# Sums of the retention heads taken on chip instead of reloaded, sums of the up layers on one engine, and a later start of the adaLN sums

## The chip, the cores and the metric

The kernel runs on one NeuronCore of a Trainium2 chip. The core has a matrix engine (TensorE, PE in the profile), three engines for elementwise work (VectorE: DVE; ScalarE: ACT; GpSimd: POOL), a SyncE (SP) that here only issues DMAs, and 16 DMA engines that move data between HBM and on-chip memory. Each engine works through its own instructions in order; engines wait for each other by semaphores. A DMA that an engine issues stands in that engine's instruction order. Matmul results land in PSUM, in 8 banks of 128x512 floats. The metric is the device time of one execution in microseconds (us), lower is better.

## What is computed

Two layers of a diffusion backbone on 1024 latent tokens of width 1024 with 256 context tokens, in float32. Cut to what the change touches:

```python
# layer 0: retention mixer (4 heads, key width 256, value width 512), then SwiGLU
o_f = retention_chunk_scan(qx, kx, vx, lg_f, s_f)            # chunks of 128 tokens
o_b = flip(retention_chunk_scan(flip(qx), flip(kx), flip(vx), lg_b, s_b))
o = o_f + o_b
o = o * rsqrt(mean(o * o, axis=-1) + EPS)                    # per head
yx = (silu(g) * o) @ w_o                                     # (1024, 2048) @ (2048, 1024)
hx = hx + g1 * yx
fx = rms_norm(hx, norm_ffn) * (1 + sc2) + sh2
hx = hx + g2 * ((silu(fx @ w1) * (fx @ w3)) @ w2)
# layer 1: the same with a gated short convolution as mixer
# sh, sc, g of both layers: silu(c) @ ada_w + ada_b  (adaLN)
return rms_norm(hx, final_norm)
```

## The kernel before, in words

**Arithmetic.** Every float32 operand is split into a high and a low part (`split`, L123 to L126: a ScalarE copy, then a subtraction on VectorE), and a product is three fast matmuls (`mm3`, L128 to L132). Most large products use a seven-product scheme of the Strassen and Winograd kind: of the four quarters of the activation, x11, x12, x21, x22, seven operands are made, three of them quarters themselves and four sums, numbered 5 (x12 - x11), 6 (x22 - that sum), 7 (sum 6 - x11) and 4 (x21 - sum 6).

**Order of the work.** The program is written as one order of TensorE work. Beside it a queue of small steps (`hooks`) is emptied one step after each product or half step, and a scheduler then places the instructions of each engine; the numbers on the tiles are names only.

**Retention stage (about 600 to 855 us).** It runs over 4 heads, and in each over 10 steps (2 of context, 8 chunks of 128 tokens), forward and backward together. `update` adds k^T v to the state in PSUM and copies it out as high and low parts: L723 on ScalarE, then L724 on VectorE. `read` multiplies queries with that copy. So every step has a round trip from TensorE to ScalarE to VectorE and back to TensorE. When a head has ended, eight `finish` steps (one for each chunk c) go through `hooks`: L769 on VectorE scales the chunk with the gate, 4 transposes on TensorE (L774) turn it, L776 on ScalarE copies it from PSUM, and L778, a DMA issued by ScalarE, stores it to `og_d[h][c // 4]` in pieces of 512 bytes.

**The sums of the heads.** The output projection `w_o` is such a seven-product layer (`down`). Its quarters: head h is 2p + i with p the pair of heads, i the first or second half of the inner dimension, and j = c // 4 the token half. In the kernel before, `o_steps` makes the four sums: `load` (L1409) reads the stored tiles back with SyncE's DMAs, `one` (L1416) and `other` (L1421, L1423, L1425) subtract on VectorE, and `put` (L1412) stores the sums to `x_d` by ScalarE's DMAs, in pieces of 2 KB. These steps are queued behind the `finish` steps of a head. `down` then reads its operands one by one (L1106, three ahead) and splits them.

**Up layers (three of them, from about 1045, 1690 and 2025 us).** `modulator` makes the normalized operands (L294, L303, then `split`); every third of them has its subtraction (L126) on GpSimd. `x_sums` makes the four sums of the seven-product scheme (L412, L416); for the odd ones of four tiles the subtractions run on GpSimd (their splits on VectorE). `winograd` makes the weights' sums (L452 to L458), and L496, L500, L506 add up products from PSUM. The first phase of the program uses `x_sums` too. `x_steps` (L1241 to L1251) makes the sums of what an up layer puts out, two tile pairs at a time, through `hooks`.

**adaLN.** `ada_next` forms scale, shift and gate vectors as row sums on VectorE (L203), two instructions of 512 columns a step, with weights loaded two steps ahead; `also` calls it after every third product of the first up layer, from its first product on.

Of the kernel before, what the change touches and what calls it, by code (L numbers as in the profile page):

```python
# [17 lines left out]
P = 128  # L18
# [33 lines left out]
def hybrid_kernel(ctx: ExitStack, tc: tile.TileContext, a: dict):  # L52
# [353 lines left out]
    def x_sums(xc, b, kt):  # L406

        x11, x12, x21, x22 = (b[kt + 4 * i, j] for i in range(2) for j in range(2))
        eng = nc.gpsimd if kt % 2 else nc.vector

        def step(n, dst, p, q):
            eng.tensor_sub(dst, p, q)  # L412
            x_parts(xc, n, kt, dst)

        def seven():
            eng.tensor_sub(x21, x21, x12)  # L416
            step(7, x12, x12, x11)

        return {
            5: lambda: step(5, x12, x12, x11),  # L420
            6: lambda: step(6, x12, x22, x12),
            7: seven,
            4: lambda: x_parts(xc, 4, kt, x21),
        }
# [97 lines left out]
    og_d = spilled("og_d", HEADS, NTB, shape=(P, 4, 512))  # L522
    x_d = spilled("x_d", 7, FT // 2)
# [242 lines left out]
    def finish(h, c):  # L766
# [6 lines left out]
        for b in range(4):  # L773
            nc.tensor.transpose(ot[:, b * P : (b + 1) * P], gt[:, b * P : (b + 1) * P], ident)  # L774
        og = ttile()
        nc.scalar.copy(og, ot)  # L776
        t0 = (c % 4) * P
        nc.scalar.dma_start(  # L778
            og_d[h][c // 4][:, :, t0 : t0 + P], og.rearrange("p (b t) -> p b t", b=4)
        )  # L780
        gate(h, c + G_AHEAD)

    def og_of(k, tb):
        return og_d[k // 4][tb][:, k % 4]
# [437 lines left out]
    def x_steps(n_pairs):  # L1222
# [8 lines left out]
        def take(pr, i, j, t):  # L1231
# [3 lines left out]
            if all((pr, i, j) in parts for i in range(2) for j in range(2)):  # L1235
# [18 lines left out]
                hooks.extend([one, two])  # L1254
# [3 lines left out]
    def modulator(xs, s, sh):  # L1258
        def one(kt, tb, rb):
# [3 lines left out]
                nc.gpsimd if kt % 3 == 1 else nc.vector,  # L1263
# [24 lines left out]
    def ffn(i, xs, w_plain, consume, order, then=(), last=False):  # L1288
# [18 lines left out]
        def also():  # L1307
            n = next(count)
            if i == 0 and n == 0:
                ada_load(ADA_EARLY)  # L1310
                ada_load(ADA_EARLY + 1)
            elif n % 3 == 0:
# [73 lines left out]

    o_ready = set()
    o_sums = {}

    def o_tile(i, n):  # L1390

        k, tb = S_X[n]
        return og_of(i // 4 * 8 + k * 4 + i % 4, tb)

    def o_src(n, i):
        if n in S_X:
            return o_tile(i, n) if (i // 4 * 2 + S_X[n][0]) in o_ready else None
        return x_d[n - 1][i] if (n, i) in o_sums else None

    def o_steps(pairs):  # L1400


        t = {}

        def load(i, k):
            r = raw()
            for tb in range(NTB):
                t[i, k, tb] = r[:, tb * TB : (tb + 1) * TB]
                nc.sync.dma_start(t[i, k, tb], og_of(i // 4 * 8 + k * 4 + i % 4, tb))  # L1409

        def put(n, i, src):
            nc.scalar.dma_start(x_d[n - 1][i], src)  # L1412
            o_sums[n, i] = True

        def one(i):
            nc.vector.tensor_sub(t[i, 0, 1], t[i, 0, 1], t[i, 0, 0])  # L1416
            put(5, i, t[i, 0, 1])

        def other(i):
            x11, x12, x21, x22 = (t.pop((i, k, tb)) for k in range(2) for tb in range(NTB))  # L1420
            nc.vector.tensor_sub(x22, x22, x12)  # L1421
            put(6, i, x22)
            nc.vector.tensor_sub(x11, x22, x11)  # L1423
            put(7, i, x11)
            nc.vector.tensor_sub(x21, x21, x22)  # L1425
            put(4, i, x21)

        def after_loads(k, f):

            todo = [lambda i=i: load(i, k) for i in pairs] + [nothing] * 2  # L1430
            sums = [nothing] * 2 + [lambda i=i: f(i) for i in pairs]

            def both(x, y):
                x()
                y()

            return [lambda x=x, y=y: both(x, y) for x, y in zip(todo, sums)]

        return after_loads(0, one), after_loads(1, other)

    o_steps = {h: o_steps(range(2 * h, 2 * h + 4)) for h in (0, 2)}
# [6 lines left out]
    for i, (r, _) in enumerate(seq):  # L1448
# [8 lines left out]
        if r is not None and r[1] == steps - 1:  # L1457
# [6 lines left out]
            hooks.append(lambda h=h: o_ready.add(h))  # L1464
            if h:
                hooks.extend(o_steps[h // 2 * 2][h % 2] if h > 1 else sum(o_steps[0], []))
# [189 lines left out]
```

## Time and profile before

| what | value |
|---|---|
| time, median of 3 runs | 2673.85 us (2672.15 to 2674.78) |
| the profiled execution's own time | 2677.7 us |
| span in its profile, first to last instruction | 2675.9 us |
| mean granted TensorE clock | 0.987 |
| busy: PE, DVE, ACT, POOL | 97%, 73%, 44%, 8% of the span |
| HBM traffic | 317.07 MB read, 111.67 MB written |

Times inside the program are us from the span's start. Busy time of TensorE counts each matmul with its drain, which overlaps the next one, so gaps show better in the number of matmuls in a window than in busy time. In a row of a timeline the brackets say how long the engine had been idle before it and what ended that. PEclk is the granted clock as a share of the full one.

### The profile page before, as it was taken

The numbers are of one execution on the slowest core, as the hardware profiler recorded it, in microseconds if no ns is written. First come the engines' busy times: TensorE is split into PE (matmuls) and PEld (weight loads), VectorE is DVE, ScalarE is ACT, GpSimd is POOL, SyncE is SP. The second block draws the span as 40 slices with busy tenths as digits, with TensorE's granted clock in tenths as the row PEclk, the third lists the DMA queues.
The fourth block names the chain that finished last, engine by engine and source line by source line (L and its number), as shares of the span: only waits on it lengthen the run. The fifth ranks groups of instructions, "written<-read, shape, count | busy, mean of one in ns | idle before, by whom it ended". The sixth has DMA issues, their size and how long they took to land.

```text
span 2675.9 us, 32892 instructions
## 1 busy us (share of the span) xinstructions
PE 2589.0 (97%) x11448; PEld 2111.6 (79%) x11448; DVE 1952.4 (73%) x3354; ACT 1187.8 (44%) x2162; POOL 203.0 (8%) x142
## 2 busy tenths in 40 slices
PE   8999999999978899999999999999998999999998
PEld 4788888887767687788888888788777888888886
DVE  4886766768877878877766877777798566667774
ACT  4643333448866345333333445433354333334452
POOL 1110221002210002000000000200002000000000
PEclk9999999999999899999999999999999999999998
DMA  9556234664679743445545734123552233328532
GB/s 328 193 165 220 79 115 165 230 227 126 207 252 309 270 127 96 156 146 179 189 132 197 266 102 152 34 81 97 177 197 73 87 110 107 101 98 305 166 98 83
DMA packets 212614, 430.93 MB, mean 161 GB/s; under 512 B 22624, under 2 KB 40160, under 8 KB 212448
## 3 DMA queue, kind: packets, MB, share of 16 engines
q1 hardware_dynamic: 139248, 318.92, 37.1%
q10 hardware_dynamic: 73200, 109.91, 11.2%
q8 instruction: 90, 1.47, 0.2%
q14 instruction: 76, 0.62, 0.1%
HBM read 317.07 MB, written 111.67 MB: 160 GB/s over the span
## 4 chain that ended last, share of the span: by engine, by line
PE 80%; DVE 8%; DMA 6%; issue 3%; ACT 2%; POOL 0%; SPq 0%; ACTq 0%; DVEq 0%; POOLq 0%
PE ps L130 26%; PE ps L131 26%; PE ps L132 26%; DVE u L126 3%; ACT u L125 1%; DMA raw<-in_w_kc 1%; DMA raw<-og_d 1%; DMA tt<-x_d 1%; DMA og_d<-tt 1%; PE ps L954 1%; DVE tt L412 1%; DVE t L294 0%; DMA tt<-in_cxT 0%; PE ps L774 0%; DVE u L724 0%
## 5 line engine op out<-in xcount | busy, mean ns | idle before, releaser
L130 PE MATMUL ps<-u 128*128 128x512 f32 x3472 | 1366.4, 394 | 46.1 <-DVE u L724 18.0
L131 PE MATMUL ps<-u 128*128 128x512 f32 x3472 | 1363.2, 393 | 1.7 <-DVE u L126 1.5
L132 PE MATMUL ps<-u 128*128 128x512 f32 x3472 | 1359.3, 392 | 0.0
L130 PEld LDWEIGHTS ps<-u 128*128 128x128 f32 x3472 | 656.1, 189 | 194.7 <-DVE u L724 21.0
L131 PEld LDWEIGHTS ps<-u 128*128 128x128 f32 x3472 | 656.9, 189 | 142.0 <-DVE u L126 6.0
L132 PEld LDWEIGHTS ps<-u 128*128 128x128 f32 x3472 | 656.7, 189 | 136.7 <-issue 0.5
L125 ACT CAST u<-raw 128x512 fp32r<-128x512 f32 x772 | 466.4, 619 | 563.9 <-PE ps L132 273.6
L126 DVE TENSOR_TENSOR u<-raw,u 128x512 fp32r<-128x512 f32 x772 | 539.5, 712 | 163.1 <-ACT u L125 161.3
L125 ACT CAST u<-tt 128x512 fp32r<-128x512 f32 x394 | 232.1, 619 | 241.1 <-issue 58.5
L126 DVE TENSOR_TENSOR u<-tt,u 128x512 fp32r<-128x512 f32 x391 | 280.0, 743 | 79.8 <-ACT u L125 77.8
L493 ACT COPY tt<-ps 128x512 f32<-128x512 f32 x174 | 101.9, 586 | 212.1 <-PE ps L132 206.4
L724 DVE SCALAR_TENSOR_TENSOR u<-ps,u 128x512 fp32r<-128x512 f32 x128 | 84.7, 685 | 26.6 <-ACT u L723 26.3
L506 DVE TENSOR_TENSOR tt<-tt,ps 128x512 f32<-128x512 f32 x58 | 39.9, 687 | 87.0 <-PE ps L132 87.0
L126 POOL TENSOR_TENSOR u<-t,u 128x512 fp32r<-128x512 f32 x15 | 21.4, 1428 | 1032.0 <-ACT u L125 1031.2
L1202 DVE SCALAR_TENSOR_TENSOR t<-ps,ada,t 128x512 f32<-128x512 f32 x80 | 56.1, 751 | 53.6 <-PE ps L132 53.6
L723 ACT ACTIVATE u<-ps 128x512 fp32r<-128x512 f32 x128 | 72.9, 597 | 39.8 <-PE ps L132 21.7
L673 POOL TENSOR_TENSOR u<-t,u 128x512 fp32r<-128x512 f32 x40 | 55.0, 1378 | 327.2 <-ACT u L672 179.9
L500 DVE TENSOR_TENSOR tt<-tt,ps 128x512 f32<-128x512 f32 x58 | 39.8, 686 | 49.1 <-ACT tt L493 48.9
L203 DVE SCALAR_TENSOR_TENSOR raw<-raw,c_row 128x512 f32<-128x512 f32 x84 | 55.2, 689 | 23.9 <-DMA raw<-in_ada_t 23.9
L130 PE MATMUL ps<-u,kh 128*128 128x512 f32 x144 | 58.2, 404 | 1.2 <-POOL u L673 1.2
L131 PE MATMUL ps<-u,kh 128*128 128x512 f32 x144 | 57.0, 396 | 0.5 <-DVE kh L683 0.5
L132 PE MATMUL ps<-u,kh 128*128 128x512 f32 x144 | 56.9, 395 | 0.0
(147 smaller groups left out, 1797.2 us busy)
## 6 DMA issues: line engine op xcount, KB each, us to landing
tt<-x_d SPq DMA_DIRECT2D x214, 256.0 KB, 3.7
raw<-in_w SPq DMA_DIRECT2D x88, 512.0 KB, 4.0
x_d<-tt ACTq DMA_DIRECT2D x130, 256.0 KB, 2.6
raw<-in_w SPq DMA_DIRECT2D x88, 256.0 KB, 5.1
raw<-in_ada_t SPq DMA_DIRECT2D x42, 512.0 KB, 5.2
t<-in_ada_t SPq DMA_DIRECT2D x76, 256.0 KB, 4.8
raw<-in_w_v SPq DMA_DIRECT2D x36, 512.0 KB, 5.0
x_d<-t ACTq DMA_DIRECT2D x52, 256.0 KB, 3.4
```

The costliest lines, as they stand in the source:

```text
L125: nc.scalar.copy(dst_hi, src)
L126: (eng or nc.vector).tensor_sub(dst_lo, src, dst_hi.bitcast(F32))
L130: nc.tensor.matmul(ps, w_hi, x_lo, start=first, stop=False, **kw)
L131: nc.tensor.matmul(ps, w_lo, x_hi, start=False, stop=False, **kw)
L132: nc.tensor.matmul(ps, w_hi, x_hi, start=False, stop=last, **kw)
L203: nc.vector.scalar_tensor_tensor(w[e], w[e], 1.0, c_row[:, k], op0=ALU.mult, op1=ALU.mult, accum_out=sums[:, e, ct : ct + 1],)
L493: nc.scalar.copy(m[p, n], ps)
L506: nc.vector.tensor_add(t, t, ps)
L673: nc.gpsimd.tensor_sub(t[:, 1], v, t[:, 0].bitcast(F32))
L723: nc.scalar.activation(s[:, 0], st[d][m], AF.Copy, scale=f)
L724: nc.vector.scalar_tensor_tensor(s[:, 1], st[d][m], f, s[:, 0].bitcast(F32), op0=ALU.mult, op1=ALU.subtract,)
L1202: nc.vector.scalar_tensor_tensor(h, banks[which][c], gate[:, kt : kt + 1], h, op0=ALU.mult, op1=ALU.add)
```

## The change

It does four things.

1. `finish` keeps the turned chunks of the first three quarters of a pair of heads on chip (`o_place`, six `raw` tiles of a pool of 38 for each pair) and subtracts as soon as the chunk that completes a sum is there: `first` (one subtraction a chunk, after the second token half of an even head), `others` (three a chunk, after the second token half of an odd head). The sums are stored to a new `os_d`, in pieces of 512 bytes, by ScalarE. The store of a sum is put off to the next chunk's `finish`. Tiles that nobody loads any more (quarter x12) are not stored, and `o_steps` with its 32 loads is gone.
2. `x_sums` and `modulator` use VectorE for all their tiles.
3. The first two steps of `x_steps` of an up layer are put off by four products (`[nothing] * 4`).
4. `also` starts the second part of the adaLN sums with product 12 instead of 0.

```diff
     def x_sums(xc, b, kt):
-        eng = nc.gpsimd if kt % 2 else nc.vector
         def step(n, dst, p, q):
-            eng.tensor_sub(dst, p, q)
+            nc.vector.tensor_sub(dst, p, q)
             x_parts(xc, n, kt, dst)
         def seven():
-            eng.tensor_sub(x21, x21, x12)
+            nc.vector.tensor_sub(x21, x21, x12)
...
+    os_d = spilled("os_d", 4, HEADS // 2, shape=(P, 4, 512))
...
-        og = ttile()
+        og, put = o_place(h, c)
         nc.scalar.copy(og, ot)
-        t0 = (c % 4) * P
-        nc.scalar.dma_start(
-            og_d[h][c // 4][:, :, t0 : t0 + P], og.rearrange("p (b t) -> p b t", b=4)
-        )
+        t = slice((c % 4) * P, (c % 4 + 1) * P)
+        def store(dst, src):
+            nc.scalar.dma_start(dst[:, :, t], src.rearrange("p (b t) -> p b t", b=4))
+        if (h % 2, c // 4) != (0, 1):
+            store(og_d[h][c // 4], og)
+        o_finish()
+        if put is not None:
+            o_late.append(lambda: put(store))
         gate(h, c + G_AHEAD)
...
+    o_parts, o_late = {}, []
+    def o_finish():
+        while o_late:
+            o_late.pop()()
+    def o_place(h, c):
+        p, i, j, c4 = h // 2, h % 2, c // 4, c % 4
+        if (i, j) == (1, 1):
+            og = ttile()
+        else:
+            if c4 % 2 == 0:
+                o_parts[p, "r"] = raw()
+            og = o_parts[p, "r"][:, (c4 % 2) * 512 : (c4 % 2 + 1) * 512]
+            o_parts[p, i, j, c4] = og
+        def first(store):
+            x11 = o_parts[p, 0, 0, c4]
+            nc.vector.tensor_sub(x11, og, x11)
+            store(os_d[0][p], x11)
+        def others(store):
+            t1, x12, x21 = (o_parts.pop((p, *k, c4)) for k in ((0, 0), (0, 1), (1, 0)))
+            nc.vector.tensor_sub(t1, og, t1)
+            store(os_d[1][p], t1)
+            nc.vector.tensor_sub(x12, og, x12)
+            store(os_d[2][p], x12)
+            nc.vector.tensor_sub(x21, x21, t1)
+            store(os_d[3][p], x21)
+        return og, {(0, 1): first, (1, 1): others}.get((i, j))
...
-                hooks.extend([one, two])
+                hooks.extend([nothing] * (4 if pr == 0 else 0) + [one, two])
...
-                nc.gpsimd if kt % 3 == 1 else nc.vector,
+                nc.vector,
...
-            if i == 0 and n == 0:
+            if i == 0 and n == 12:
                 ada_load(ADA_EARLY)
                 ada_load(ADA_EARLY + 1)
-            elif n % 3 == 0:
+            elif n > 12 and n % 3 == 0:
                 ada_next()
...
-    def o_steps(pairs):
...
-    o_steps = {h: o_steps(range(2 * h, 2 * h + 4)) for h in (0, 2)}
...
-            hooks.append(lambda h=h: o_ready.add(h))
-            if h:
-                hooks.extend(o_steps[h // 2 * 2][h % 2] if h > 1 else sum(o_steps[0], []))
+            hooks.extend([o_finish, lambda h=h: o_ready.add(h)])
```

**Three places in the engines' order.** Line numbers of the changed kernel stand in its rows: L780 is the store in `finish` (L778 before), L816, L818, L820 are the subtractions of `others`, L495 is L496 before, L451 to L457 are L452 to L458, L1283 and L1287 are L1244 and L1248.

ScalarE at the `finish` steps of head 1, between two pairs of state copies (L723). Before:

```order
L723 ACTIVATE u<-ps 128x512 x2
L672 CAST u<-t_6413 128x512
L682 ACTIVATE kh<-tt,kdec 128x256
L125 CAST u<-tt 128x512
L776 COPY tt<-ps 128x512 x2
L778 DMA og_d_1_218<-tt 512x1x128 x2
L747 ACTIVATE t_6629<-ps,odec 128x512
L723 ACTIVATE u<-ps 128x512 x2
```

Now, the part just ahead of the later pair:

```order
L125 CAST u<-tt 128x512
L776 COPY tt<-ps 128x512
L780 DMA os_d_0_225<-raw 512x1x128
L780 DMA og_d_1_218<-tt 512x1x128
L780 DMA os_d_0_227<-raw 512x1x128
L780 DMA os_d_0_229<-raw 512x1x128
L776 COPY tt<-ps 128x512
L780 DMA os_d_0_225<-raw 512x1x128
L780 DMA og_d_1_218<-tt 512x1x128
L780 DMA os_d_0_227<-raw 512x1x128
L780 DMA os_d_0_229<-raw 512x1x128
L747 ACTIVATE t_6653<-ps,odec 128x512
```

Two stores between two pairs have become twelve (four more stand ahead of these rows).

SyncE behind the gates (g_d) of head 1. Before:

```order
L763 DMA tt<-g_d_7_190 128x512
L1409 DMA raw<-og_d_0_215 128x512
L1409 DMA raw<-og_d_1_216 128x512
L1409 DMA raw<-og_d_0_215 128x512
L652 DMA tt<-k_d_3_128 128x512
L1409 DMA raw<-og_d_1_216 128x512
L1409 DMA raw<-og_d_0_215 128x512
L1409 DMA raw<-og_d_1_216 128x512
L652 DMA tt<-k_d_0_125 128x512
L1409 DMA raw<-og_d_0_215 128x512
L1409 DMA raw<-og_d_1_216 128x512
L652 DMA t_6752<-v_d_8_173 128x512
```

Now:

```order
L763 DMA tt<-g_d_7_190 128x512
L652 DMA tt<-k_d_3_128 128x512
L652 DMA t_6764<-v_d_8_173 128x512
L652 DMA t_6766<-v_d_9_174 128x512
L652 DMA tt<-k_d_0_125 128x512
L652 DMA t_6829<-v_d_0_165 128x512
L652 DMA t_6864<-v_d_7_172 128x512
L652 DMA tt<-k_d_4_134 128x512 x2
```

The keys and values of the next head no longer stand behind loads of stored tiles.

VectorE ahead of the first L496 of the first up layer. Before:

```order
L454 TENSOR_TENSOR raw<-raw 128x512
L1241 TENSOR_TENSOR tt<-tt 128x512
L456 TENSOR_TENSOR raw<-raw 128x512
L1300 TENSOR_TENSOR tt<-tt,ps 128x512
L126 TENSOR_TENSOR u<-raw,u 128x512 x2
L1244 TENSOR_TENSOR t_9610<-tt 128x512
L203 SCALAR_TENSOR_TENSOR t_9577,ada<-t_9577,c_row 128x512
L1248 TENSOR_TENSOR tt<-t_9610,tt 128x512
L1251 TENSOR_TENSOR t_9633<-tt,t_9610 128x512
L203 SCALAR_TENSOR_TENSOR t_9578,ada<-t_9578,c_row 128x512
L458 TENSOR_TENSOR raw<-raw 128x512
L496 TENSOR_TENSOR tt<-tt,ps 128x512
```

Now:

```order
L453 TENSOR_TENSOR raw<-raw 128x512
L451 TENSOR_TENSOR raw<-raw 128x512
L455 TENSOR_TENSOR raw<-raw 128x512
L126 TENSOR_TENSOR u<-raw,u 128x512
L495 TENSOR_TENSOR tt<-tt,ps 128x512
L126 TENSOR_TENSOR u<-raw,u 128x512 x2
L457 TENSOR_TENSOR raw<-raw 128x512
L126 TENSOR_TENSOR u<-raw,u 128x512
L1283 TENSOR_TENSOR t_9618<-tt 128x512
L1287 TENSOR_TENSOR tt<-t_9618,tt 128x512
```

The sums of `x_steps` and the adaLN sums have moved behind it; further ahead eight sums and two splits of GpSimd's have joined the queue. From the four L281 that begin the stage to this L496 VectorE has 57, 52 and 56 instructions in the three up layers before, and 62, 61 and 62 now.

## Rows read from the trace of the kernel before

**Rows 1.** The page, its first part: busy us (share of the span), x instructions.
```profile
PE 2589.0 (97%) x11448; PEld 2111.6 (79%) x11448; DVE 1952.4 (73%) x3354; ACT 1187.8 (44%) x2162; POOL 203.0 (8%) x142
```

**Rows 2.** Waits of TensorE, whole program: us in total, times, longest us.
```profile
PE ps L130 <- DVE u L724: 18.0, 6, 7.7
...
PE ps L130 <- DVE tt L496: 14.1, 4, 5.6
...
PE ps L774 <- DVE tt L769: 7.7, 7, 2.2
```

**Rows 3.** Windows of 40 us: us, busy (x) of each engine, PEclk, DMA, GB/s.
```profile
760.00:800.00 40.00, 27.05 (x103) 20.44 (x103) 32.11 (x61) 22.78 (x49) 7.95 (x6) 0.87 0.72 236
...
800.00:840.00 40.00, 33.57 (x157) 26.71 (x157) 30.55 (x48) 27.97 (x57) 5.75 (x5) 0.99 0.88 287
...
840.00:880.00 40.00, 36.43 (x161) 29.18 (x162) 28.77 (x55) 20.02 (x42) 0.00 (x0) 0.92 0.98 336
...
880.00:920.00 40.00, 31.03 (x107) 23.49 (x106) 29.44 (x48) 12.89 (x24) 0.00 (x0) 0.83 0.91 322
...
1080.00:1120.00 40.00, 34.36 (x143) 27.69 (x142) 34.40 (x72) 15.70 (x28) 0.00 (x0) 0.91 0.49 158
...
1120.00:1160.00 40.00, 40.00 (x179) 33.12 (x178) 29.06 (x55) 14.49 (x26) 0.00 (x0) 1.00 0.46 152
...
1720.00:1760.00 40.00, 37.26 (x164) 30.36 (x163) 35.82 (x60) 17.99 (x33) 0.85 (x1) 1.00 0.27 86
...
2040.00:2080.00 40.00, 34.97 (x143) 28.15 (x142) 35.31 (x48) 16.93 (x31) 9.87 (x6) 0.91 0.22 73
```

**Rows 4.** TensorE timeline near 776 us; chain row of eight transposes (start, us).
```profile
776.05 0.80 PE L130 MATMUL ps<-u 128*128 128x512 f32 x1 [7.67 <-DVE u L724]
...
804.35 0.88 PE ps L774 x8
```

**Rows 5.** VectorE timeline near 764 and 774 us.
```profile
764.69 0.69 DVE L1421 TENSOR_TENSOR raw<-raw 128x512 f32<-128x512 f32 x1 [1.68 <-DMA raw<-og_d]
...
773.98 0.69 DVE L1421 TENSOR_TENSOR raw<-raw 128x512 f32<-128x512 f32 x1 [4.29 <-DMA raw<-og_d]
```

**Rows 6.** ScalarE timeline, its store issues (ACTq) and a state copy.
```profile
740.67 1.22 ACTq L778 DMA_DIRECT2D og_d<-tt  x2
...
771.99 1.08 ACT L723 ACTIVATE u<-ps 128x512 fp32r<-128x512 f32 x2 [5.47 <-DMA x_d<-raw]
...
890.41 8.62 ACTq L1412 DMA_DIRECT2D x_d<-raw  x8
```

**Rows 7.** DMA view, ScalarE's queue q10 alone, 655:745, then 888:912: packets, MB, share.
```profile
q10 hardware_dynamic: 7681, 3.82, 14.7%
...
q10 hardware_dynamic: 1728, 3.15, 34.0%
```

**Rows 8.** SyncE, ScalarE and VectorE timelines, 812 to 889 us.
```profile
812.51 8.13 SPq L1409 DMA_DIRECT2D raw<-og_d  x3
...
837.71 0.62 ACT L125 CAST u<-tt 128x512 fp32r<-128x512 f32 x1 [1.15 <-DMA tt<-og_d]
...
888.26 1.51 DVE L1421 TENSOR_TENSOR raw<-raw 128x512 f32<-128x512 f32 x2 [5.27 <-DMA raw<-og_d]
```

**Rows 9.** VectorE and GpSimd timelines, 1045 to 1092 us.
```profile
1045.26 2.06 DVE L294 SCALAR_TENSOR_TENSOR tt<-tt,ada,ps 128x512 f32<-128x512 f32 x3 [3.20 <-PE ps L289]
...
1061.75 1.89 DVE L126 TENSOR_TENSOR u<-tt,u 128x512 fp32r<-128x512 f32 x3
...
1063.12 1.67 POOL L412 TENSOR_TENSOR tt<-t,tt 128x512 f32<-128x512 f32 x1 [5.38 <-DVE u L126]
...
1063.56 1.78 DVE L412 TENSOR_TENSOR tt<-t,tt 128x512 f32<-128x512 f32 x1
...
1091.22 0.69 DVE L496 TENSOR_TENSOR tt<-tt,ps 128x512 f32<-128x512 f32 x1
```

More of the change, by code (lines that the diff above doesn't have):

```diff
@@ L774, in finish @@
             nc.tensor.transpose(ot[:, b * P : (b + 1) * P], gt[:, b * P : (b + 1) * P], ident)
-        og = ttile()
+        og, put = o_place(h, c)
         nc.scalar.copy(og, ot)
-        t0 = (c % 4) * P
-        nc.scalar.dma_start(
-            og_d[h][c // 4][:, :, t0 : t0 + P], og.rearrange("p (b t) -> p b t", b=4)
-        )
-        gate(h, c + G_AHEAD)
-    def og_of(k, tb):
-        return og_d[k // 4][tb][:, k % 4]
+        t = slice((c % 4) * P, (c % 4 + 1) * P)
[6 more added lines that the diff above has]
+            o_late.append(lambda: put(store))
+        gate(h, c + G_AHEAD)
+    o_parts, o_late = {}, []
[24 more added lines that the diff above has]
+        return og, {(0, 1): first, (1, 1): others}.get((i, j))
     seq = [(None, [(0, n) for n in range(NCX)])]
@@ L1387, in hybrid_kernel @@
     o_ready = set()
[L1388 to L1393, printed above, removed]
     def o_src(n, i):
-        if n in S_X:
-            return o_tile(i, n) if (i // 4 * 2 + S_X[n][0]) in o_ready else None
-        return x_d[n - 1][i] if (n, i) in o_sums else None
-    def o_steps(pairs):
[L1403 to L1439, printed above, removed]
-    o_steps = {h: o_steps(range(2 * h, 2 * h + 4)) for h in (0, 2)}
+        p, b = i // 4, i % 4
+        k, tb = S_X.get(n, (0 if n == 5 else 1, 0))
+        if 2 * p + k not in o_ready:
+            return None
+        src = og_d[2 * p + k][tb] if n in S_X else os_d[{5: 0, 6: 1, 7: 2, 4: 3}[n]][p]
+        return src[:, b]
     fx, w_plain = {}, {}
```

## The prediction

> **What bounds the kernel now.** I read the page first: TensorE is busy for 97% of the span, GpSimd for 8% [rows 1]. No other engine is the bound overall, so time can only be won where TensorE stands still or runs slowly. The view of waits says where that is: 18.0 us for the state copy L724, 14.1 us for L496, 7.7 us for the gated chunk L769 [rows 2]. The windows then price each place, because they count matmuls and show the granted clock. In an undisturbed window 179 matmuls take 40 us, 0.2235 us each [rows 3]. A transpose of 128 columns takes 0.11 us [rows 4], half of that. What a window lacks of 179 is lost, idle time and half clock together:
>
> - 760 to 800: 103 matmuls, 17.0 us lost.
> - 800 to 840: 157, of them most of a head's 32 transposes (28 taken), 8.0 us.
> - 840 to 880: 161, with another head's 32 transposes, 7.6 us.
> - 880 to 920: 107, 16.1 us.
> - 1080, 1720 and 2040: 143, 164 and 143, so 8.0, 3.4 and 8.0 us [rows 3].
>
> These are 48.7 us around the heads and 19.4 us at the up layers, 68 us that the change can reach. The clock was at 0.83 in the 880 window: after such a wait TensorE starts at the lower of its two levels, 1.2 GHz, as its 0.80 us matmul after 7.67 us of idleness shows [rows 3, 4].
>
> **The heads' stalls.** The longest wait ends with L724 at 776 us [rows 4]. L724 was late because VectorE stood 1.68 and 4.29 us for `raw<-og_d`, the tiles loaded back, with L724 behind them in its order [rows 5], while ScalarE stood 5.47 us behind the stores of the sums, with the state copy L723 behind those [rows 6]. SyncE took 8.13 us over three such loads at 812 us, and the projection's loads stood behind them; ScalarE then waited for its first operand (1.15 us) and L723 waited with it. At 888 us VectorE had stood 5.27 us for the last loaded tiles [rows 8].
>
> **Part 1, the sums on chip.** Removed are 32 loads, 8 stores and the waits for both; the 32 subtractions remain (4 of `first` and 4 x 3 of `others` for each of two pairs). The 32 stores of sums remain, in 512-byte pieces. Place by place:
>
> - 760 to 800: nothing in head 2's first steps waits for a stored tile any more. An undisturbed head passage loses next to nothing, so I take 15 of the 17.0 us, bounds 8 and 17.
> - 800 to 880: the three loads' 8.13 us leave SyncE's order, so the projection's first operands come some 10 us earlier and the stop near 840 us goes. The gates' chunks (7.7 us of waits for L769 in all heads) stay. I take 8 of 15.6 us, bounds 2 and 12.
> - 880 to 920: the 5.27 us wait goes, and what head 3 adds to operands 6, 7 and 4 is needed only behind product 5, which alone takes 8 x 12 = 96 matmuls, 21 us. But ScalarE now has head 3's 20 stores, at 0.61 us each (two in 1.22 us) [rows 6], in the same 20 us as the splits of the operands. I take 11 of 16.1 us, bounds 3 and 15.
> - Head 1, new: between two pairs of state copies ScalarE's order has ten more stores. At 0.61 us that is 6.1 us, at the rate of eight stores in 8.62 us under full DMA load 10.8 us [rows 6], and nothing if reads and transposes cover it. The near row is the 0.61 us one, since the loads that filled the DMA engines are gone; with 2 us for the clock I take +8 us, bounds 0 and 14.
> - Heads 0 and 2: four subtractions each, 4 x 0.60 = 2.4 us on VectorE. I take +1 us for both, bounds 0 and 5.
>
> DMA time: a queue of only 512-byte packets took 0.147 x 90 x 16 / 7681 = 0.028 us per packet, one of 1.8 KB packets 0.34 x 24 x 16 / 1728 = 0.076 us [rows 7]. A 256 KB store then costs 0.88 us of all 16 engines instead of 0.68. The change takes away 32 loads (0.68 to 0.88 us each) and 8 stores and adds 32 x 0.20 = 6 us: 23 to 29 us less in a stretch where the DMA share was 0.72 to 0.98 [rows 3].
>
> The Trainium skill speaks against this part: "Perfetto Trace Analysis", section DMA Optimizations, says that small DMAs, under 2 KB, carry a large overhead per transfer. Read on the pieces of a DMA, and with the large pieces' price for each, the rule would give the third rival's store instead of the 0.88 us; the rows bear it out only in part, since a 512-byte packet took 0.37 of a large one's time.
>
> Sum of part 1: -15 - 8 - 11 + 8 + 1 = **-25 us**.
>
> **Part 2, the up layers.** From L294 at 1045.26 to L496 at 1091.22 us VectorE needed 46.0 us for 57 instructions, though three in a row start 0.60 us apart [rows 9]; 57 x 0.60 = 34.2. In that stretch GpSimd works on eleven (three splits of `modulator`, eight sums), and a VectorE instruction that meets one takes 1.78 us instead of 0.69: L412 at 1063.56 ends only after GpSimd's, which ran from 1063.12 for 1.67 us [rows 9]. Eleven times 1.09 us are 12.0, about the 11.8 us that are too many. So each instruction moved costs VectorE 0.60 us and gives back 1.09. Now 62 instructions stand ahead of L496 (the adaLN and `x_steps` ones have moved behind it): 37.2 us, some 8 us earlier. The wait there was at most 5.6 us [rows 2], so L496 is then no longer last; next would be the operands' and weights' splits right behind it, which TensorE needs one product (some 2.7 us, 12 matmuls) at a time. The other two up layers have 61 and 62 instructions instead of 52 and 56: +5.4 and +3.6 us, against some 12 us given back. I take 14 of the 19.4 us, bounds 3 and 18. The same page of the Trainium skill, section Optimizing Scalar/DVE Operations, says that work may go to GPSIMD when VectorE is saturated, and that this may not help since both share a read port. By its first half the second rival would come, by its second half this part; the row pair at 1063 us speaks for the second half.
>
> The first phase gets 8 sums more on VectorE, 4.8 us, beside 8.7 us given back, under TensorE work without gaps: 0. The adaLN sums start 12 products later; 38 steps, one every three products, end with product 126 of 140, ahead of their use: 0, bounds 0 and 2.
>
> **Sum.** 2677.7 (the profiled execution) - 25 - 14 = 2638.7 us. The profile lies 3.85 us above the median of the runs, so I predict a median of 2635 us.
>
> **Rivals.**
>
> 1. ScalarE's order takes the place of the loads. The stores of head 1 and head 3 stand ahead of state copies and operand splits; at 1.08 us each they cost 14 us in head 1 and keep 13 of the 16.1 us at head 3, and half of part 2 comes. -15 - 4 - 3 + 14 + 3 - 10 = -15: 2659. For it: the order rows, with twelve stores between two pairs. Against it: the DMA engines have less to do.
> 2. VectorE is the bound in the up layers. If the stretched instructions come from something other than GpSimd, L496 is later by 5, 9 and 6 instructions, 20 x 0.60 = 12 us, instead of 14 earlier: -25 + 12 = -13: 2661. Against it: the coincidence in rows 9.
> 3. Small packets, the slower side. If a packet of any size cost what the large ones took, a store would take 512 x 0.076 / 16 = 2.4 us, and the 32 new ones 77 us of DMA time against 22: +55, with up to 30 removed. The DMA engines stay full, the gates and projection loads are as late as now, and the 25 us more stand on TensorE's path: +25 - 14 = +11: 2685. It decides from about 1.7 us a store on, where the added DMA time (32 x 1.0) is as large as what is removed. Against it: rows 7.
> 4. No change. The chunks hold six more tiles of the pool while a pair lasts, the projection's weights get theirs later, and the wait moves from loaded sums to weights; part 2 finds another wait just behind: 2674.
> 5. Nearly everything goes: bounds of part 1 at -44 + 1 and of part 2 at -17: 2614.
>
> **How the numbers follow.** Forecast 0.49 (own range 2622 to 2648), rival 1 0.21, rival 2 0.09, rival 3 0.05, rival 4 0.05, rival 5 0.11. The range should leave out rivals 3 and 4 and a little at the ends: 2612 to 2665. Within 0.2% is 5.3 us, about what a measurement can tell. Faster: 0.49 + 0.21 + 0.09 + 0.11 = 0.90, less 0.02 for a mixture of them that comes out at or above no change: 0.88. Same 0.05 + 0.01, slower 0.05 + 0.01.
>
> **What would show it.** Right: no VectorE wait for a DMA around 760 us, the 760 window above 160 matmuls; L496 off the list of long waits; GpSimd's busy time down by some 80 us (50 instructions of up to 1.67 us). Wrong step in part 1: L723 or L724 as releaser of waits at 730 to 745 us with ScalarE full of store issues. Wrong in part 2: the same number of matmuls in the 1080 and 2040 windows, with L126 as releaser. The prediction as a whole is wrong if the windows from 760 to 920 still lack over 35 us.

## The result, and the profile after

| | before | changed |
|---|---|---|
| time, median (4 runs each) | 2674.3 us (2672.2 to 2678.1) | 2656.9 us (2653.2 to 2658.5) |
| ratio, 95% interval | | 0.9931 (0.9914 to 0.9948) |
| span of the profiled execution | 2675.9 us | 2651.4 us |

The change is worth 18 us (14 to 23), a gain, inside the range, but less than half of the 39 us that the sum held. Of all runs in this document one, the second of e4, took 3242.6 us at a granted clock of 0.75, and e4's figures leave it out.

The page of the changed kernel, part 1. It answers to [rows 1]: fifty instructions have left GpSimd, whose busy time falls by 78.5 us. VectorE has fifty more and is yet 7.5 us less busy.

```profile
PE 2580.5 (97%) x11448; PEld 2108.8 (80%) x11448; DVE 1944.9 (73%) x3404; ACT 1191.6 (45%) x2162; POOL 124.5 (5%) x92
```

What TensorE waited for, whole program (us in total, times, longest), against [rows 2]. L496, now L495, is off the list and L724 has shrunk from 18.0 to 7.4 us. At the top stands L126, the low part of an operand split, with one wait of 10.4 us.

```profile
PE ps L130 <- DVE u L126: 17.0, 5, 10.4
...
PE ps L130 <- DVE u L724: 7.4, 6, 3.3
...
PE ps L774 <- DVE tt L769: 4.6, 4, 1.4
```

The windows, against [rows 3]. The up layers' three are full. Of the heads' windows 760 is nearly full, but those at 720 and 840 have lost matmuls (175 and 161 before; the first row is that of the kernel before, the rest are the changed kernel's).

```profile
720.00:760.00 40.00, 37.28 (x175) 29.15 (x174) 30.92 (x52) 28.22 (x58) 8.63 (x6) 1.00 0.84 271
...
720.00:760.00 40.00, 32.27 (x141) 25.49 (x141) 31.75 (x50) 24.46 (x48) 7.26 (x5) 0.91 0.83 260
760.00:800.00 40.00, 37.98 (x175) 30.36 (x173) 34.28 (x63) 31.51 (x69) 9.86 (x7) 1.00 0.57 178
800.00:840.00 40.00, 34.84 (x150) 28.02 (x151) 30.65 (x50) 28.08 (x61) 4.36 (x3) 0.96 0.89 292
840.00:880.00 40.00, 29.89 (x136) 23.12 (x134) 28.56 (x55) 10.67 (x21) 0.00 (x0) 0.90 0.88 276
880.00:920.00 40.00, 34.31 (x130) 27.14 (x131) 32.07 (x53) 19.50 (x37) 0.00 (x0) 0.84 0.63 192
1080.00:1120.00 40.00, 40.00 (x178) 33.12 (x177) 29.19 (x52) 14.05 (x25) 0.00 (x0) 1.00 0.47 152
1720.00:1760.00 40.00, 40.00 (x178) 33.12 (x177) 30.45 (x52) 15.53 (x27) 0.00 (x0) 1.00 0.30 99
2040.00:2080.00 40.00, 40.00 (x178) 33.15 (x177) 29.16 (x47) 19.08 (x34) 0.00 (x0) 1.00 0.29 95
```

Windows slide over the program when a kernel gets faster. For the heads I therefore timed the same points of the program in each trace: the first transposes of each head's `finish` steps, and the first product with `ones` that follows the projection. Before, TensorE's timeline, head 3's first transposes and that product:

```profile
861.29 0.66 PE L774 MATMUL ps<-ident,tt 128*128 128x128 f32 x4
...
990.35 0.95 PE L263 MATMUL ps<-ones,tt 128*128 128x1 f32 x8
```

After, the same two:

```profile
847.91 0.66 PE L774 MATMUL ps<-ident,tt 128*128 128x128 f32 x4
...
982.81 0.95 PE L263 MATMUL ps<-ones,tt 128*128 128x1 f32 x8
```

So head 3's `finish` steps begin 13.4 us earlier, and 5.8 of these are lost again by the end of the projection (134.9 us instead of 129.1). All heads read in this way, with the kernels of the experiments:

| us between these points | before | changed | e1 | e13 | e2 | e5 | e6 | e3 |
|---|---|---|---|---|---|---|---|---|
| head 0 to head 1 | 57.7 | 57.8 | 57.7 | 57.7 | 57.8 | 57.8 | 57.7 | 57.7 |
| head 1 to head 2 | 75.3 | 67.9 | 75.9 | 72.4 | 64.7 | 69.4 | 62.9 | 64.6 |
| head 2 to head 3 | 62.9 | 58.5 | 63.3 | 65.3 | 57.4 | 59.8 | 57.4 | 57.4 |
| head 3 to product with ones | 129.1 | 134.9 | 126.0 | 119.5 | 119.9 | 122.7 | 116.3 | 111.9 |

**Where head 3 loses.** TensorE's timeline. It stands 10.4 us until a split is done, and comes back at the lower clock: the matmul takes 0.76 us instead of 0.40, and the granted clock of the two windows here is 0.90 and 0.84.

```profile
872.24 0.40 PE L132 MATMUL ps<-u 128*128 128x512 f32 x1
883.03 0.76 PE L130 MATMUL ps<-u 128*128 128x512 f32 x1 [10.40 <-DVE u L126]
```

ScalarE's timeline in the same stretch (ACTq rows are its DMA issues, the time from start to end of a merged row includes what lies between them):

```profile
857.65 1.21 ACTq L780 DMA_DIRECT2D og_d<-tt  x2
860.87 5.35 ACTq L780 DMA_DIRECT2D os_d<-raw  x3
866.26 0.62 ACT L125 CAST u<-tt 128x512 fp32r<-128x512 f32 x1 [8.09 <-DMA og_d<-tt]
...
870.48 0.52 ACTq L780 DMA_DIRECT2D og_d<-tt  x1
...
872.50 0.59 ACT L776 COPY tt<-ps 128x512 f32<-128x512 f32 x1 [4.62 <-DMA os_d<-raw]
...
876.18 0.52 ACTq L780 DMA_DIRECT2D og_d<-tt  x1
877.52 3.98 ACTq L780 DMA_DIRECT2D os_d<-raw  x2
881.55 0.62 ACT L125 CAST u<-tt 128x512 fp32r<-128x512 f32 x1 [8.47 <-DMA og_d<-tt]
```

The splits' first half (L125) stands still for 8.09 and 8.47 us behind stores, and a copy (L776) for 4.62. A single issue takes 0.52 us, but these 21.2 us went by behind thirteen stores, 1.63 us each; the longest hold is in the row at 877.52, two issues in 3.98 us, so that the second held ScalarE for 3.46. The chain of waits tells what the stores waited for, an earlier transfer's landing (here of stores):

```profile
862.29 8.11 DMA os_d<-raw
...
870.48 5.63 DMA og_d<-tt
...
876.18 7.13 DMA og_d<-tt
...
883.40 0.32 SPq L1145
...
883.76 6.00 DMA raw<-in_w_o
...
889.78 0.70 DVE raw L1159
...
890.51 0.63 ACT u L125
```

The chain goes on from the third store's landing to SyncE, where a load of a sum (L1145) had waited for it, with a load of the projection's weights behind that. TensorE's next wait, 2.62 us up to 891.22, hangs on these weights. So the stores held up loads as well, not the splits alone.

The stores' wait is written into the program. The listing of ScalarE's instructions, with their waits (rows between are left out):

```
886 L780 DMA os_d_1_228<-raw 512x1x128 [waits DMAHW6_49,DVE_49]
...
892 L780 DMA og_d_1_222<-tt 512x1x128 [waits DMAHW6_49,Activation_49]
...
897 L780 DMA og_d_1_222<-tt 512x1x128 [waits DMAHW6_49,Activation_49]
...
900 L125 CAST u<-tt 128x512
```

The transfers of ScalarE and SyncE get one of eight counters, DMAHW0 to 7, in turn (each counter ends 168 or 169 of the 1350 transfers in the trace). In this program a transfer waits on its engine until the last user of its counter has landed; this is called a store's turn below. Row 886 is issued at 862.29 and lands 8.11 us later, row 892 starts then, row 897 5.63 us after that. The cast in row 900 has no wait of its own; it stands behind all of them.

### The profile page after: what moved, and what is told of

It is laid out like the page before. It is cut to its first block, busy times and chain, and to the rows that moved or that the text cites. A ratio compares the mean times of both kernels' runs of the same rounds, so it can differ in the third digit from the quotient of the medians.

```text
span 2651.4 us, 32772 instructions
## 1 busy us (share of the span) xinstructions
PE 2580.5 (97%) x11448; PEld 2108.8 (80%) x11448; DVE 1944.9 (73%) x3404; ACT 1191.6 (45%) x2162; POOL 124.5 (5%) x92
## 4 chain that ended last, share of the span: by engine, by line
PE 87%; DVE 5%; DMA 4%; issue 2%; ACT 1%; ACTq 0%; POOL 0%; SPq 0%; DVEq 0%; POOLq 0%
PE ps L130 28%; PE ps L131 28%; PE ps L132 28%; DVE u L126 1%; PE ps L993 1%; DVE u L724 1%; DMA og_d<-tt 0%; DVE kh L683 0%; DMA tt<-x_d 0%; DMA raw<-in_xT 0%; DMA raw<-in_w_kc 0%; PE ps L289 0%; DMA tt<-in_cxT 0%; ACT u L125 0%; PE ps L774 0%
## 5 line engine op out<-in xcount | busy, mean ns | idle before, releaser
L125 ACT CAST u<-raw 128x512 fp32r<-128x512 f32 x772 | 466.7, 620 | 536.4 <-PE ps L132 277.4
L126 DVE TENSOR_TENSOR u<-raw,u 128x512 fp32r<-128x512 f32 x772 | 535.9, 707 | 157.2 <-ACT u L125 152.1
L125 ACT CAST u<-tt 128x512 fp32r<-128x512 f32 x394 | 233.1, 619 | 235.2 <-issue 56.9
L126 DVE TENSOR_TENSOR u<-tt,u 128x512 fp32r<-128x512 f32 x394 | 264.6, 695 | 87.8 <-ACT u L125 85.6
L492 ACT COPY tt<-ps 128x512 f32<-128x512 f32 x174 | 102.2, 588 | 211.6 <-PE ps L132 202.8
L724 DVE SCALAR_TENSOR_TENSOR u<-ps,u 128x512 fp32r<-128x512 f32 x128 | 84.2, 684 | 28.1 <-ACT u L723 27.9
L723 ACT ACTIVATE u<-ps 128x512 fp32r<-128x512 f32 x128 | 73.2, 598 | 29.5 <-PE ps L132 27.9
L673 POOL TENSOR_TENSOR u<-t,u 128x512 fp32r<-128x512 f32 x40 | 55.9, 1402 | 319.4 <-ACT u L672 161.4
L961 ACT COPY tt<-ps 128x512 f32<-128x512 f32 x48 | 28.1, 587 | 63.5 <-PE ps L132 62.6
```

What stands on the lines that cost most here:

```text
L125: nc.scalar.copy(dst_hi, src)
L126: (eng or nc.vector).tensor_sub(dst_lo, src, dst_hi.bitcast(F32))
L492: nc.scalar.copy(m[p, n], ps)
L673: nc.gpsimd.tensor_sub(t[:, 1], v, t[:, 0].bitcast(F32))
L723: nc.scalar.activation(s[:, 0], st[d][m], AF.Copy, scale=f)
L724: nc.vector.scalar_tensor_tensor(s[:, 1], st[d][m], f, s[:, 0].bitcast(F32), op0=ALU.mult, op1=ALU.subtract,)
```

## The experiments

All were timed beside the kernel before on the same chip; gains below are (1 - ratio) x 2675 us. "Changed" is the kernel under study.

**e1: the heads as before.** The part of the change on `finish`, `o_place`, `o_finish` and `o_steps` is undone; the rest stays.

> Heads as before (their sums from tiles loaded back); the sums of the up layers on VectorE alone and the later adaLN as in the changed kernel. The forecast's split (heads 25 us, up layers 14 us) would put this at 2657 + 25 = 2682 us, slower than before, or, held against the kernel before, at 2674 - 14 = 2660 us. What TensorE lost by 20-us stretches in the two traces (heads, 700 to 920: 52.8 us before, about 47 after; stretches at 1080, 1720, 2060: 19 us before, none after) says 2663 us (2659 to 2667): the up layers gave nearly all of the gain and the heads some 6 us. The rival, that the heads gave nothing or cost time, says 2657 us or below.

Measured: 2658.7 us, ratio 0.9936 (0.9923 to 0.9948), a gain of 17 us; the changed kernel gains 18. The heads' rework as a whole is worth 1 us in the timed runs, give or take 6 (both intervals); in the traces, by the columns' sums, 4 to 6 us. The up layers brought nearly everything.

**e2: the stores of sums from GpSimd.**

```diff
-        def store(dst, src):
-            nc.scalar.dma_start(dst[:, :, t], ...
+        def store(dst, src, eng=nc.scalar):
+            eng.dma_start(dst[:, :, t], ...
...
-            o_late.append(lambda: put(store))
+            o_late.append(lambda: put(lambda dst, src: store(dst, src, nc.gpsimd)))
```

> The 32 stores of the sums (os_d) are issued by GpSimd and not by ScalarE; nothing else changes. Theory A, ScalarE's order: each store on ScalarE waits there until an earlier transfer has landed (8.1 us and 5.6 us in the chain of waits at 862 to 882), and the operand splits stand behind it; then the 23 us that TensorE loses at 860 to 900 fall to 10 or less, head 1 gives 2 to 5 us, and the time is 2643 us (2638 to 2648). Theory B, the transfers themselves: DMA engines are over 0.9 busy at 860 to 900, with 512-byte packets, so the operands arrive late whoever issues the stores; then the time is 2654 to 2659 us and the splits wait for their tiles instead.

Measured: 2636.8 us, 0.9852 (0.9839 to 0.9866), a gain of 40 us. This is theory A, and more than it expected.

**e3: no stores of sums.**

```diff
-            store(os_d[0][p], x11)
...
-            store(os_d[1][p], t1)
...
-            store(os_d[2][p], x12)
...
-            store(os_d[3][p], x21)
...
-        src = og_d[2 * p + k][tb] if n in S_X else os_d[{5: 0, 6: 1, 7: 2, 4: 3}[n]][p]
+        src = og_d[2 * p + k][tb]
```

The sums are still made, but the projection reads tiles of og_d in their place.

> The 32 stores of the sums are left out, and the operand loads of the four sums read tiles of og_d in their place (as many loads of the same size; the output is not the reference's). This bounds what the stores cost by any road. Theory A: about as fast as with the stores on GpSimd, 2640 us (2634 to 2645). Theory B: clearly faster than with the stores on GpSimd, 2640 us against 2656. If TensorE still loses 20 us or more at 860 to 900, neither holds and the loads or the tile pools are what binds there: 2655 us.

Measured: 2628.6 us, 0.9821 (0.9808 to 0.9834), a gain of 48 us, more than either theory had said. Its window shows that busy DMA engines alone stop nothing: their share is 0.90, as in the changed kernel (0.88), and 191 matmuls and transposes run instead of 136, at full clock.

```profile
840.00:880.00 40.00, 39.94 (x191) 32.66 (x190) 36.71 (x69) 17.85 (x35) 0.00 (x0) 1.00 0.90 286
```

By itself e3 against e2 left 8 us for the transfers (theory B). e6 took that away.

**e4: head 3's last stores later.**

```diff
-            o_late.append(lambda: put(store))
+            (o_tail if h == HEADS - 1 else o_late).append(lambda: put(store))
...
+            if h == HEADS - 1:
+                hooks.extend(lambda i=i: o_tail[i]() for i in range(4))
+                hooks.append(lambda: o_ready.add("tail"))
```

> Only head 3's last four groups (three subtractions and three stores each) come later: after the last transpose of head 3, into the products of the second of the seven parts of the layer, which need none of them. Theory A: the splits for the first products no longer stand behind twelve stores; the wait of 10.4 us near 872 goes or shrinks below 4, and some of it comes back a product later because the stores still stand in ScalarE's order: 2650 us (2645 to 2655). Theory B: the same bytes in the same 40 us: 2655 to 2659 us.

Measured: 2649.6 us, 0.9898 (0.9883 to 0.9913), as theory A expected. The wait at 872 us is gone, but one of 4.66 us has come at 889.9. ScalarE's casts waited 15.4 us in two pieces behind stores (wait list, 700 to 920):

```profile
ACT u L125 <- DMA os_d<-raw: 15.4, 2, 8.4
```

Delay moves the block; it does not take it away.

**e5: only head 3's twelve stores from GpSimd.** As e2, for `(h, c // 4) == (HEADS - 1, 1)` alone.

> As the changed kernel, but of the 32 stores of sums only the last 12, of head 3, are issued by GpSimd; the other 20 stay on ScalarE. With all 32 on GpSimd the time fell by some 20 us, and TensorE's lost time at 860 to 900 from 23.2 to 7.9 us. Theory A1, that the block is head 3's twelve stores ahead of the operand splits: 2657 - 15 = 2642 us (2639 to 2646). The rival, that what helps is fewer transfers in the ring of counters shared by ScalarE's and SyncE's queues everywhere, or head 1's stores: about 12 of 32 parts of it, 2649 us (2647 to 2653).

Measured: 2644.8 us, 0.9884 (0.9868 to 0.9900): 13 of the 21 us between the changed kernel and e2. The block is mainly at head 3 (12.2 us of the table's last line, 134.9 to 122.7); of the rest the most lies from head 1 to head 2 (69.4 against 64.7).

**e6: the stores of sums from SyncE.** As e2, with `nc.sync` in place of `nc.gpsimd`.

> All 32 stores of sums are issued by SyncE, off ScalarE's order but in the order of the loads, and with the same eight shared counters. Theory A1, ScalarE's order alone: the splits are free of the stores, 2645 us (2640 to 2650), unless the loads that now stand behind a store's wait for VectorE come late. The rival, the shared counters and the transfers in flight: the waits move from ScalarE to SyncE and the tiles come late by as much, 2655 to 2662 us.

Measured: 2628.0 us, 0.9825 (0.9811 to 0.9840), a gain of 47 us and as fast as without the stores (e3). The transfers are the same, in the same small pieces, with the same eight counters; only the engine that waits for their turns is another. Thus the place in ScalarE's order cost 28 us. The traffic of the stores cost nothing that the timed runs can tell (by the columns' sums e3 lies 2.6 us below e6), and theory B has fallen. Windows of e6:

```profile
840.00:880.00 40.00, 36.77 (x172) 28.79 (x171) 31.78 (x54) 16.13 (x29) 0.00 (x0) 1.00 0.95 285
880.00:920.00 40.00, 40.00 (x179) 33.10 (x178) 40.00 (x67) 21.60 (x41) 0.00 (x0) 1.00 0.63 200
```

The DMA share in the first is higher than after the change (0.95 against 0.88), and the clock stays at 1.00. The loads that stand behind SyncE's stores do come late: ScalarE's casts wait 5.12 and 3.42 us for `tt<-os_d` at 868 and 874 us, but TensorE waits for at most 1.42 us at a time there.

**e7: head 3's stores of og_d from GpSimd too.** As e2, with `store(og_d[h][c // 4], og, nc.gpsimd if h == HEADS - 1 else nc.scalar)`.

> All 32 stores of sums and head 3's eight stores of og_d are issued by GpSimd, which has no other work by then. Against the kernel with the 32 stores on GpSimd (2637 us): theory A1 gives back part of the 7.9 us that TensorE still loses at 860 to 880, where a copy and a split waited for transfers on ScalarE: 2632 us (2629 to 2636). If those waits are for the loads of tiles, it is the same, 2637 us.

Measured: 2627.4 us, 0.9820 (0.9807 to 0.9834), 9 us better than e2: the eight stores that had stayed on ScalarE held it up as well. In e2 the last four of them landed after a median of 13.7 us, and ScalarE stood 6.33 us for one of them; in e7, from GpSimd, they land after 7.3 us at most. ScalarE's timeline in e2, and the DMA view from 840 to 880 us, of e2 and then of e6:

```profile
867.55 0.59 ACT L776 COPY tt<-ps 128x512 f32<-128x512 f32 x1 [6.33 <-DMA og_d<-tt]
...
og_d<-tt ACTq DMA_DIRECT2D x4, 256.0 KB, 13.7
...
og_d<-tt ACTq DMA_DIRECT2D x4, 256.0 KB, 6.8
```

**e8: the up layers' sums and the modulation back on GpSimd.** The changes to `x_sums` and `modulator` are undone; heads, empty steps and adaLN as in the changed kernel.

> As the changed kernel, but the up layers' sums and modulation are put back on GpSimd for the tiles that had it; the four empty steps and the later adaLN stay. In the trace the 19 us that TensorE lost at 1080, 1720 and 2060 are all gone with the change. Theory: GpSimd's subtractions of 1.1 us and VectorE's that meet them (1.8 us against 0.7) delayed the weights' sums, so this loses 12 to 19 us: 2672 us (2668 to 2676). The rival, that the four empty steps alone moved those sums ahead: 2658 us (2655 to 2661).

Measured: 2673.0 us, 0.9990 (0.9981 to 0.9999): 16 us slower than the changed kernel. The wait on L496 (here L497) is back; waits of TensorE:

```profile
PE ps L130 <- DVE tt L497: 13.1, 3, 5.2
```

VectorE's timeline in it: four subtractions of the splits take 5.78 us where GpSimd works beside them (three of its subtractions from 1060.78 to 1066.45, 1.62 to 1.68 us each and not the expectation's 1.1), and 2.48 us soon after.

```profile
1061.22 5.78 DVE L126 TENSOR_TENSOR u<-tt,u 128x512 fp32r<-128x512 f32 x4
...
1071.03 2.48 DVE L126 TENSOR_TENSOR u<-tt,u 128x512 fp32r<-128x512 f32 x4
```

**e9: the modulation alone back on GpSimd.** `nc.gpsimd if kt % 3 == 1 else nc.vector` in `modulator`.

> As the changed kernel, but the modulation is put back on GpSimd for every third tile; the up layers' first sums stay on VectorE. With modulation and first sums both back the time was 2673 us, 16 us more than the changed kernel's, with the wait on the weights' sums (5.2 us) back at 1080. If the first sums held GpSimd and VectorE up there, this is near the changed kernel, 2657 us (2654 to 2661), or a little faster, since VectorE has less to do ahead of the norm's product (2.0 us at 1030 where it was 1.1). If the modulation did, it is 2670 us (2666 to 2674).

Measured: 2652.3 us, 0.9913 (0.9899 to 0.9927). The whole gain of the up layers is that of `x_sums`. Moving the modulation as well gave nothing and may have cost 4 to 5 us. The intervals of e9 and of the changed kernel overlap, and beside e6 the same move is worth 1 us (e14).

**e10: without the four empty steps.** `hooks.extend([one, two])`.

> As the changed kernel, but without the four empty steps ahead of the first pair's sums in the two kinds of down layers. They are not in the way of the sums at 1080 in the forecast's account, so they are worth nothing there: 2657 us (2654 to 2660). The rival: they hold VectorE's sums back while it has operands to split, and without them a wait of 2 to 5 us comes: 2662 us.

Measured: 2657.1 us, 0.9929 (0.9917 to 0.9942). The empty steps are worth nothing.

**e11: adaLN at its old place.** `n == 0` and `n % 3 == 0` in `also`.

> As the changed kernel, but the second group's adaLN products start at step 0 of the up layer as before, not behind step 12. The forecast put the shift at 0: 2657 us (2654 to 2660). The rival: with VectorE doing all sums of the up layer's first steps, adaLN's products there come between those and the wait on the weights' sums comes back at 1080 to 1120: 2663 us (2660 to 2667).

Measured: 2656.3 us, 0.9924 (0.9910 to 0.9937). The place is worth nothing.

**e12: sums from SyncE, head 3's og_d from GpSimd.**

> Meant as the fastest: the 32 stores of sums are issued by SyncE (2628 us so far) and head 3's eight stores of og_d by GpSimd (which gave some 9 us beside the stores of sums on GpSimd). TensorE still loses 4.6 us at 860 to 880 with SyncE's stores, where splits wait for tiles loaded from os_d (5.1 and 3.4 us) and not for a store's turn. Theory A1: only the stores' turns are taken away, and few are left: 2626 us (2622 to 2629). If the og_d stores of head 3 still hold the splits up by 4 us or more, 2623 us or below.

Measured: 2631.6 us, 0.9835 (0.9822 to 0.9849), no better than e6 or e7. The two moves do not add up.

**e13: the heads as before, their sums' stores from SyncE.** e1, and in `put`:

```diff
-            nc.scalar.dma_start(x_d[n - 1][i], src)
+            nc.sync.dma_start(x_d[n - 1][i], src)
```

> The kernel with the heads as before (2659 us), but the 32 stores of their sums, there 128 pieces of 2 KB each, are issued by SyncE. With the new heads the same move took 2657 to 2628 us. Theory A1: the old heads' cost was in loads that came back late (TensorE lost 15 and 9 us where a split or a state waited) and not in ScalarE's turns, so this gains little: 2657 us (2652 to 2663). The rival, that the place of the stores alone is worth 20 us or more to either way of making the sums: 2637 us or below, and the new heads are worth nothing by themselves.

Measured: 2648.4 us, 0.9897 (0.9880 to 0.9913), between the two expectations. With e1, the changed kernel and e6 it makes a square of gains over the kernel before:

| sums' stores on | ScalarE | SyncE |
|---|---|---|
| old heads | 17 us (e1) | 28 us (e13) |
| new heads | 18 us (changed) | 47 us (e6) |

So the new heads are worth 19 us where the stores are off ScalarE and 1 us where they are on it. The old heads lost to their stores' place too, some 10 us.

**e14: e6 and e9 together.**

> The changed kernel with the stores of sums on SyncE (2628 us) and the modulation back on GpSimd for every third tile (which took 2657 to 2652 us). The two lie 100 us apart on the way, so they should add up: 2624 us (2620 to 2627). If the modulation's gain was a shift in the heads' stores, it is 2628 us.

Measured: 2626.9 us, 0.9819 (0.9805 to 0.9834). The intervals of e6, e7 and e14 overlap almost wholly. The runs don't order these three; any of them beats both kernels, by about 1.1% the changed one.

## Why the prediction was right or wrong

**The heads, forecast -25, got -1 (timed runs) to -6 (traces).** The step that failed is the term 880 to 920, and in it the price of a store on ScalarE at head 3: 0.61 us was taken, 1.63 us were measured. Against the points of the table:

- Heads 0 and 2, forecast +1: nothing seen at head 0 (57.7 and 57.8); head 2's part lies inside the stretch to head 3.
- 760 to 800 (-15) and head 1 (+8): together -7 forecast, -7.4 measured (75.3 to 67.9). The loaded tiles' wait went, and the sign that was named for head 1 came a little behind its place: at 749.68 TensorE had waited 3.28 us for L724, and ScalarE's work ahead of the state copy had stood 2.43 us behind stores (rows below: TensorE's timeline, then ScalarE's). Here the stores waited for no turn. They follow each other at some 0.7 us, near the forecast's 0.61, and in the trace every counter had come free before. With the stores on SyncE this stretch takes 62.9 us, so of the +8 some 5 us were their place on ScalarE.

```profile
749.68 0.79 PE L130 MATMUL ps<-u 128*128 128x512 f32 x1 [3.28 <-DVE u L724]
```

```profile
744.79 0.57 ACTq L780 DMA_DIRECT2D os_d<-raw  x1
745.46 0.61 ACTq L780 DMA_DIRECT2D og_d<-tt  x1
746.16 1.47 ACTq L780 DMA_DIRECT2D os_d<-raw  x2
747.73 0.69 ACT L747 ACTIVATE t<-ps,odec 128x512 f32<-128x512 f32 x1 [2.43 <-DMA os_d<-raw]
```

- 800 to 920 (-8 and -11): this failed. From head 2 to head 3 came -4.4, and behind that +5.8. The step is the one on 880 to 920, "ScalarE now has head 3's 20 stores, at 0.61 us each", for which -11 was taken with bounds of -3 and -15. The 0.61 us is the time of an issue. At head 3 a store held ScalarE until its turn had come and the issue was done, 1.63 us on average for the thirteen above and up to 3.46 us, and the splits' first halves stood behind it. At head 1 a store of ScalarE landed after a median of 3.5 us, before its counter was needed again; at head 3, from 857 to 882 us, after 6.9. e5 gives 13 us for twelve of these stores alone, e6 28 us for all 32. Where they cost nothing, in e6, the column lies 31 us below that of before; the forecast without its +8 for stores was -33.

The Trainium skill, "Perfetto Trace Analysis", section DMA Instruction — HWDGE (DVE, Sync), says that what the profiler shows of such an issue begins only when its semaphores are satisfied, and that the sequencer is free for the next instruction only behind it. The row at 877.52 agrees: two issues of 0.52 us each in 3.98 us, with nothing else of ScalarE between them.

The signs had been there. In [rows 6] L723 stood 5.47 us and its releaser was a DMA `x_d<-raw`, a store of ScalarE's own, and eight stores took 8.62 us. I read both as the DMA engines being full and expected them to go with the loads. They were turns: the five stores ahead of that L723 took 4.17 us, where an issue of theirs takes 0.33; in the trace four of them waited for their counter, which twice a store of ScalarE and twice a load of SyncE set free. e13 shows that the stores' place cost the old heads some 10 us. ScalarE's timeline before:

```profile
767.77 4.17 ACTq L1412 DMA_DIRECT2D x_d<-raw  x5
```

**Part 2, forecast -14, got -17 (e1) and -16 (e8).** Right in place and mechanism: the 1080, 1720 and 2040 windows filled, which is the 19.4 us that they had lacked, less small waits elsewhere. e9 narrows it to `x_sums`. The price of a meeting, 1.09, holds: in e8 four VectorE instructions that met three of GpSimd's took 3.30 us longer (5.78 against 2.48), 1.10 us a meeting. As a price for every moved instruction it was too high: VectorE is 7.5 us less busy with fifty more instructions of 0.60 us, so each gave back about (30 + 7.5) / 50 = 0.75 us, an estimate that takes in whatever else changed on VectorE. That some met none of VectorE's would explain it; this was not counted. The zero for adaLN holds (e11), and the empty steps, which have no price in the prediction, were worth nothing (e10). The first phase was not tried by itself.

**The rivals.** The first came nearest, 2659, with a chance of 0.21: ScalarE's order took the place of the loads. That its number came so near is partly luck, since its errors cancel: it gave the stretch from head 1 to head 2 -1 us where -7.4 came and part 2 -10 where -16 to -17 came, and it let head 3 give back 3 us where 5.8 were lost. The second (VectorE the bound) is refuted by e8. The third, small packets, is refuted by e6 and e3: 32 stores in 512-byte pieces, issued from SyncE, cost no time that the timed runs can tell (2628.0 us with them, 2628.6 without). The fourth (no change) lies outside the interval. The fifth, 2614, did not come either, though e6, e7 and e14 get within 14 us of it. The Trainium skill ("Perfetto Trace Analysis", section DMA Optimizations) says that small DMAs, under 2 KB, carry a significant overhead for each transfer; here that had no price in the kernel's time. The Trainium skill also says (the same page, section Optimizing Scalar/DVE Operations) that VectorE and GpSimd share a read port, so that moving work between them might not help. e8 agrees: 5.78 us beside GpSimd for four instructions that take 2.48.

**The whole.** The sum missed by 22 us. In the two traces it missed by 14.5 (24.5 us gained of 39), and the term 880 to 920, -11 forecast and +5.8 measured, is more than all of that. The other 7.5 us are the two profiled executions: that of before was taken as 3.85 us above its kernel's median, that of the changed kernel lies 3.6 us below. The sign given for a wrong prediction was that the heads' windows still lack over 35 us. With 64 transposes counted half, 760 to 920 lack (4 x 179 - 591 + 32) x 0.2235 = 35 us (175 + 150 + 136 + 130 = 591): just at it. The sign leaves out the 720 window, where head 1's loss fell, from 175 to 141. With the stores priced at the 28 us that e6 found, which no row of before gave, the heads would have stood at -33 + 28 = -5, and the sum at 2677.7 - 5 - 14 - 3.85 = 2655 us.

## What to carry to other kernels

Price a DMA on a compute engine by what it waits for ahead of its issue, not only by the length of its issue row: in the engine's order, find which earlier transfer frees its turn, see whether that one will have landed by then, and list what stands behind. At head 1 the issue row was the right price, at head 3 it was 1 us too low for each store. Where the work behind is urgent, put the stores on a queue whose engine has nothing urgent, before counting bytes: here one word changed 28 us, and taking the stores out altogether gave no more. And when a stall is put down to its nearest releaser, read what that releaser is: a compute engine that stands behind its own store is telling of its order first, and of traffic only by way of the landing.

## What the runs showed that was not expected

- Equally busy DMA engines went with a standstill in one kernel and with none in another. From 850 to 890 us their share is 1.00 in the changed kernel, 1.00 in e6 and 0.93 in e3, and 101, 163 and 186 matmuls and transposes run. The share did not tell the bound. The three windows, in this order:

```profile
850.00:890.00 40.00, 25.52 (x101) 18.86 (x99) 21.93 (x35) 13.96 (x26) 0.00 (x0) 0.79 1.00 309
...
850.00:890.00 40.00, 36.84 (x163) 29.01 (x163) 34.90 (x58) 17.22 (x32) 0.00 (x0) 1.00 1.00 311
...
850.00:890.00 40.00, 40.00 (x186) 32.89 (x186) 39.49 (x65) 19.23 (x36) 0.00 (x0) 1.00 0.93 312
```

- GpSimd as the issuing engine was 9 us slower than SyncE (e2 and e6), though it had little else to do. The 28 stores of sums between 700 and 900 us landed after a median of 6.7 us from GpSimd and of 4.5 us from SyncE, and a cast waited up to 8.08 us for a tile of os_d, with SyncE 5.12. But this is not the cause: in e7 the median is 7.1 and the wait 8.18 us, and e7 is as fast as e6. What goes with the 9 us is ScalarE's late stores of og_d (rows at e7). Why they land so late beside GpSimd's stores was not tried.
- TensorE's wait for GpSimd's split of the values, L673, grew from 1.2 to 4.7 us (before, then the changed kernel), and e6 has it too. No experiment looked at it.

```profile
PE ps L130 <- POOL u L673: 1.2, 2, 0.7
...
PE ps L130 <- POOL u L673: 4.7, 2, 2.4
```

- e12 was expected to be the fastest, and lies 4 us behind e6 and e7; the intervals overlap, and no cause was looked for.
